# Moving the unit matrix and the ones to other start bytes in SBUF, in a two-layer decoder trunk

## The chip, the cores and the metric

The kernel runs on one core of one Trainium2 chip. The metric is the device time of one execution in microseconds (us), as the median of several runs of the same program.

## The reference

The input is one sequence of 256 tokens with 2048 channels in float32. Two layers follow each other: a gated DeltaNet layer (GDN) and an HGRN2 layer, each followed by a SwiGLU feed-forward part (FFN). Every part is normalised ahead and added to the residual, and a last normalisation ends the trunk.

```python
for layer in range(DEPTH):                      # DEPTH = 2
    if layer % N_MIXERS == 0:
        h = h + gdn_mixer(rmsnorm(h, gdn_norm[j]), ...)
    else:
        h = h + hgrn2_mixer(rmsnorm(h, hgrn_norm[j]), ...)
    h = h + swiglu(rmsnorm(h, ffn_norm[layer]), ...)
return rmsnorm(h, final_norm)
```

Both mixers project the normalised input with a large weight matrix, run a recurrence over the tokens in chunks of 64, normalise each head, multiply by a gate and project back with an output matrix. `swiglu` is `(silu(h @ w_gate) * (h @ w_up)) @ w_down`. Nearly all of the arithmetic lies in these products with weights.

## The kernel before, in words

All weights are read from HBM in pieces of 128x1024 float32 (`raw`). Each piece is split in two parts whose sum it is: ACT writes the high part `wh`, rounded to the type that TensorE takes in one pass (fp32r), and VectorE writes the low part `wl = raw - wh`. The activations are split in the same way (`xt_h`, `xt_l`; `hth`, `htl`; `ot_h`, `ot_l`). A product with weights is then three products on TensorE: high with high, high with low, low with high.

There are two ways in which the main stream issues them. `mm_rows` (L624) holds 128 tokens of the activations as the stationary operand and streams 512 columns of weights past it. `mm_cols` (L652) holds 128 columns of weights and streams all 256 tokens past them; it serves the projections whose results are wanted with channels on the partitions: `k` and `q` of the GDN layer and the first two of the four projections of each HGRN group. In the profile a product is named out<-moving,stationary, so `main<-xt_h,wh` with 256 columns is `mm_cols`, and `main<-wh,xt_h` with 512 columns is `mm_rows`. The weight buffers have their start bytes set by padding (`PAD`, `IN_COLS`, `make` at L446): 32 modulo 512 where weights are streamed, 108 (`wh`) and 364 (`wl`) where `mm_cols` holds them.

```python
PAD = 64
IN_COLS = {"wh": 108, "wl": 364}
```

Between the products of the main stream TensorE does small ones into other PSUM tiles (`aux`): the work of the recurrences, and transpositions. A transposition holds a 128x128 block of the data and streams the 128x128 unit matrix past it. `make_xt` (L716) transposes the layer's input `x` in this way, eight blocks at a time, four times for each of four norms; `head_out` (L1184) transposes the gated result `zs` of a head group, eight blocks at a time, for eight GDN groups and four HGRN groups:

```python
nc.tensor.transpose(
    tr[:, h * T + tt * P : h * T + (tt + 1) * P],
    zs[:, tt, (2 * b + h) * P : (2 * b + h + 1) * P], self.ident,
)
```

The unit matrix `self.ident` is the first 128 columns of the tile `head`, which is loaded once; its other 64 columns are norm weights. VectorE reads it too, to take diagonals (L1029) and to scale it into `vjunk` (L702). The tile `ones` is used by ten products that begin the program, as the stationary operand of four products with `vjunk` in two of the `make_rstd` calls (L705), and, one column of it, as the moving operand of the sums of squares in `gdn_qk` (L1024, `aux<-ones,sq`).

A recording layer keeps every operation, and a planner then puts all of them in an order, engine by engine, by its own costs and due times. The operations are issued from one line (L490), so that the profile shows this line for all of them, and groups are told apart by the names of their tiles. The constants lie in one pool and take their place in SBUF in the order in which `setup` (L535) declares them, each rounded up to 32 bytes per partition.

Of the kernel before, what the change touches and what calls it, by code (L numbers as in the profile page):

```python
# [17 lines left out]
P = 128  # L18
T = 256
# [487 lines left out]
class Trunk:  # L507
# [27 lines left out]
    def setup(self):  # L535
        nc, c = self.nc, self.const
        t = lambda shape, tag, dt=F32: self.tile(c, shape, tag, dt)
        self.x_home = self.tile(self.dram, [T, D], "x_home", bufs=1)
        self.x_at, self.x = self.a["x"], {}
        head = t([P, P + 64], "head")  # L540
        nc.sync.dma_start(head, self.a["head"])
        nc.ops[-1].lag = 2.4
        self.queue = [nc.ops[-1]]
        self.ident = head[:, 0:P]
        self.norms = head[:, P : P + 64].rearrange("p (n c) -> p n c", n=4)
        self.ones = t([P, P], "ones")
        nc.gpsimd.memset(self.ones, 1.0)
        self.neghalf = t([P, 8], "neghalf")
        nc.gpsimd.memset(self.neghalf, -0.5)
        self.rstd = t([P, 2], "rstd")  # L550
        self.rstdh = t([P, 2], "rstdh")
        self.rstd_row = t([P, T], "rstd_row")
        self.ssp = t([P, 2, 4], "ssp")
        self.ss = t([P, 2], "ss")
        self.junk = t([P, 512], "junk")
        self.vjunk = t([P, 256], "vjunk")
        self.xt_h = [t([P, 4, T], f"xt_h{i}", F32R) for i in range(4)]
        self.xt_l = [t([P, 4, T], f"xt_l{i}", F32R) for i in range(4)]

# [1201 lines left out]
```

## Time and profile before

| | |
|---|---|
| median of 3 runs | 2769.56 us (2769.43 to 2770.02) |
| profiled execution | 2768.12 us |
| its span, first to last instruction | 2766.0 us |
| mean granted TensorE clock | 0.999 |
| memory traffic | 580.52 MB by DMA, mean 210 GB/s |

The profile is of one execution. Busy times are sums over the span; products on TensorE overlap each other in the records, so that the distance from the start of one to the start of the next tells its price, not its own duration. The views used are the page's busy times and chain, the list of who waited for whom, the groups of instructions by name, the chain in order of time (merged pieces with their count), the timeline, and counts in chosen stretches. Times of day are us from the start of the span.

### The profile page before, as it was taken

How to read it: one execution, taken by the hardware profiler on the slowest of the kernel's cores; microseconds unless marked ns; L12 is line 12 of the kernel's file. 1: busy time of each engine (PE TensorE's matmuls, PEld its weight loads, DVE VectorE, ACT ScalarE, POOL GpSimd, SP SyncE). 2: the span in 40 equal slices, each digit the busy share in tenths (PEclk: the TensorE clock that was granted, in tenths of full speed). 3: DMA queues.
4: the chain of work that ended last, by engine and by line, in shares of the span. 5: the costliest groups of instructions: out<-in, count | busy, mean ns of one | idle time of the engine just before them, and what ended most of it. 6: DMA issues, size and time to landing. Idle time of an engine off the chain costs nothing.

```text
span 2766.0 us, 41091 instructions
## 1 busy us (share of the span) xinstructions
PE 2749.6 (99%) x15662; PEld 2333.5 (84%) x15662; DVE 1899.9 (69%) x2857; ACT 1428.6 (52%) x2010; POOL 251.6 (9%) x370
## 2 busy tenths in 40 slices
PE   9999999999999999999999999999999999999998
PEld 9888888888888888888888989988888888888887
DVE  7787888877766667446675688778657675456764
ACT  6646666565554444344444556556454444344443
POOL 1213222232110000000000100000100000000000
PEclk9999999999999999999999999999999999999999
DMA  7686668687776666676667655555776666766664
GB/s 262 201 282 222 189 213 286 205 276 218 229 254 202 193 194 194 224 223 195 192 191 224 219 163 175 168 166 176 231 258 195 193 193 209 224 208 194 195 200 160
DMA packets 162677, 580.52 MB, mean 210 GB/s; under 512 B 20138, under 2 KB 21306, under 8 KB 162352
## 3 DMA queue, kind: packets, MB, share of 16 engines
q1 hardware_dynamic: 138912, 503.15, 57.0%
q0 software_dynamic: 23280, 73.91, 8.5%
q8 instruction: 122, 2.00, 0.3%
q10 hardware_dynamic: 288, 0.85, 0.1%
q14 instruction: 75, 0.61, 0.1%
HBM read 550.52 MB, written 27.31 MB: 209 GB/s over the span
## 4 chain that ended last, share of the span: by engine, by line
PE 99%; ACT 0%; DVE 0%; issue 0%; DMA 0%; SPq 0%; POOLq 0%; POOL 0%; ACTq 0%
PE main L490 92%; PE aux L490 6%; ACT dec L490 0%; DMA first<-in_x 0%; DVE wl L490 0%; ACT wh L490 0%; DVE utmp L490 0%; SPq L490 0%; DVE pre L490 0%; ACT xt_h L490 0%; DVE u L490 0%; ACT y L490 0%; POOLq L1757 0%; ACT junk L490 0%; DVE xl L490 0%
## 5 line engine op out<-in xcount | busy, mean ns | idle before, releaser
L490 DVE TENSOR_TENSOR wl<-raw,wh 128x1024 fp32r<-128x1024 f32 x945 | 1160.7, 1229 | 755.6 <-ACT wh L490 742.2
L490 ACT ACTIVATE wh<-raw 128x1024 fp32r<-128x1024 f32 x945 | 1000.8, 1060 | 1226.9 <-PE main L490 1126.3
L490 PE MATMUL main<-wh,xt_h 128*128 128x512 f32 x2176 | 849.3, 390 | 0.8 <-ACT wh L490 0.8
L490 PE MATMUL main<-wl,xt_h 128*128 128x512 f32 x2176 | 848.4, 390 | 1.3 <-DVE wl L490 1.3
L490 PE MATMUL main<-wh,xt_l 128*128 128x512 f32 x2176 | 849.5, 390 | 0.0
L490 PEld LDWEIGHTS main<-wl,xt_h 128*128 128x128 f32 x2176 | 408.5, 188 | 85.7 <-DVE wl L490 1.6
L490 PEld LDWEIGHTS main<-wh,xt_h 128*128 128x128 f32 x2176 | 408.5, 188 | 85.0 <-ACT wh L490 1.2
L490 PEld LDWEIGHTS main<-wh,xt_l 128*128 128x128 f32 x2176 | 408.6, 188 | 84.4
L490 PE MATMUL main<-xt_h,wh 128*128 128x256 f32 (+1 forms) x1040 | 290.5, 279 | 0.7 <-ACT wh L490 0.7
L490 PE MATMUL main<-xt_h,wl 128*128 128x256 f32 (+1 forms) x1040 | 290.1, 279 | 1.0 <-DVE wl L490 0.9
L490 PE MATMUL main<-xt_l,wh 128*128 128x256 f32 (+1 forms) x1040 | 290.0, 279 | 0.3 <-DVE xt_l L490 0.3
L490 PE MATMUL main<-wh,htl 128*128 128x512 f32 x664 | 258.6, 389 | 0.0
L490 PE MATMUL main<-wl,hth 128*128 128x512 f32 x664 | 258.3, 389 | 0.0
L490 PE MATMUL main<-wh,hth 128*128 128x512 f32 x664 | 258.3, 389 | 0.0
L490 PEld LDWEIGHTS main<-xt_h,wl 128*128 128x128 f32 (+1 forms) x1040 | 194.5, 187 | 1.5 <-DVE wl L490 1.4
L490 PEld LDWEIGHTS main<-xt_h,wh 128*128 128x128 f32 (+1 forms) x1040 | 194.5, 187 | 1.3 <-ACT wh L490 0.9
L490 PEld LDWEIGHTS main<-xt_l,wh 128*128 128x128 f32 (+1 forms) x1040 | 194.5, 187 | 1.0 <-DVE xt_l L490 0.5
L490 DVE STREAM_TRANSPOSE turned<-h 32x256 f32<-32x256 f32 x352 | 153.5, 436 | 7.2
L490 PE MATMUL main<-wh,ot_l 128*128 128x512 f32 x384 | 151.2, 394 | 0.0
L490 PE MATMUL main<-wh,ot_h 128*128 128x512 f32 x384 | 150.6, 392 | 0.0
L490 PE MATMUL main<-wl,ot_h 128*128 128x512 f32 x384 | 150.5, 392 | 0.0
L490 PEld LDWEIGHTS main<-wh,hth 128*128 128x128 f32 x664 | 124.7, 188 | 25.9
(206 smaller groups left out, 2249.0 us busy)
## 6 DMA issues: line engine op xcount, KB each, us to landing
raw<-in_ffn_gu SPq DMA_DIRECT2D x352, 512.0 KB, 4.7
raw<-in_ffn_d SPq DMA_DIRECT2D x176, 512.0 KB, 4.7
raw<-in_hgrn_in SPq DMA_DIRECT2D x128, 512.0 KB, 4.1
raw<-in_gdn_kq SPq DMA_DIRECT2D x64, 512.0 KB, 5.4
raw<-in_gdn_v SPq DMA_DIRECT2D x64, 512.0 KB, 4.7
raw<-in_gdn_z SPq DMA_DIRECT2D x64, 512.0 KB, 4.9
raw<-in_gdn_out SPq DMA_DIRECT2D x64, 512.0 KB, 5.0
x_home<-x POOLq DMA_DIRECT2D x36, 512.0 KB, 6.7
```

What stands on the lines that cost most here:

```text
L490: getattr(getattr(tc.nc, op.eng), op.method)(*args, **kw)
```

## The change

`setup` declares the constants in another order and makes two of them larger, of which the kernel uses the same part as before. The tiles keep their contents; every instruction and its order on each engine stay. The place in SBUF changes, in bytes per partition, and with it the byte modulo 512:

| tile | first byte before (modulo 512) | after (modulo 512) |
|---|---|---|
| `head`, begins with the unit matrix | 16512 (128) | 16928 (32) |
| `ones` | 17280 (384) | 17696 (288) |
| `neghalf` | 17792 (384) | 16512 (128) |
| `rstd_row` | 17888 (480) | 18208 (288) |
| `junk` | 18976 (32) | 19232 (288) |
| `vjunk` | 21024 (32) | 21280 (288) |
| `rstd`, `rstdh`, `ssp`, `ss` | (416, 448, 480, 0) | (416, 448, 480, 0) |
| `xt_h0` and everything behind it | 22048 (32) and on | 512 bytes further, so the same |

```diff
@@ setup @@
         self.x_at, self.x = self.a["x"], {}
+        neghalf = t([P, 72], "neghalf")
+        self.neghalf = neghalf[:, 0:8]
+        self.rstd = t([P, 2], "rstd")
+        self.rstdh = t([P, 2], "rstdh")
+        self.ssp = t([P, 2, 4], "ssp")
+        self.ss = t([P, 2], "ss")
         head = t([P, P + 64], "head")
         nc.sync.dma_start(head, self.a["head"])
...
         self.ones = t([P, P], "ones")
         nc.gpsimd.memset(self.ones, 1.0)
-        self.neghalf = t([P, 8], "neghalf")
+        self.rstd_row = t([P, T], "rstd_row")
+        self.junk = t([P, 512], "junk")
+        self.vjunk = t([P, 320], "vjunk")[:, 0:256]
         nc.gpsimd.memset(self.neghalf, -0.5)
-        self.rstd = t([P, 2], "rstd")
-        self.rstdh = t([P, 2], "rstdh")
-        self.rstd_row = t([P, T], "rstd_row")
-        self.ssp = t([P, 2, 4], "ssp")
-        self.ss = t([P, 2], "ss")
-        self.junk = t([P, 512], "junk")
-        self.vjunk = t([P, 256], "vjunk")
         self.xt_h = [t([P, 4, T], f"xt_h{i}", F32R) for i in range(4)]
```

## The prediction

> **What bounds the kernel now.** I read the page's busy times and the chain first, then the waits, then TensorE's products one by one.
>
> ```profile
> span 2766.0 us, 41091 instructions
> PE 2749.6 (99%) x15662; PEld 2333.5 (84%) x15662; DVE 1899.9 (69%) x2857; ACT 1428.6 (52%) x2010; POOL 251.6 (9%) x370
> PE 99%; ACT 0%; DVE 0%; issue 0%; DMA 0%; SPq 0%; POOLq 0%; POOL 0%; ACTq 0%
> ```
>
> TensorE is busy 99% of the span, and the chain that ended last is TensorE's own queue. The list of who waited for whom says in which direction the weights are late:
>
> ```profile
> ACT wh L490 <- PE main L490: 1126.3, 754, 6.3
> PE main L490 <- DVE wl L490: 2.2, 2, 1.3
> ```
>
> ACT waits 1126.3 us, in 754 waits, for TensorE to hand back a weight buffer; TensorE's main stream waits 2.2 us for VectorE. What TensorE saves therefore reaches the end, unless the saving is more than the weights are ahead. So the question is whether a change of addresses alters the pace of TensorE's queue, and the chain in order of time shows that this pace isn't the same everywhere. Around the HGRN layer (start, length, piece, number of products):
>
> ```profile
> 1548.64 0.87 PE aux L490 x8
> 1549.51 7.20 PE main L490 x60
> 1556.71 0.44 PE aux L490 x4
> 1557.15 42.99 PE main L490 x338
> ...
> 1645.69 13.07 PE main L490 x115
> 1658.77 0.87 PE aux L490 x8
> 1659.64 40.62 PE main L490 x302
> ...
> 1759.75 40.62 PE main L490 x302
> ...
> 1859.87 40.62 PE main L490 x302
> ```
>
> In the pieces of 60 and 115 there are nothing but products of 256 columns (the stages that `mm_cols` issues): 7.20 us / 60 is 0.1200 us each, 13.07 / 115 is 0.1137. Same shape, same stage, 6% apart. The pieces of 302 and of 338 run from the 256-column stage into the next stage of 512 columns. The count of products in equal stretches inside the 256-column stages says the same (stretch; length, busy, products touched, granted clock, DMA share, GB/s):
>
> ```profile
> 1660.00:1690.00 30.00, 30.00 (x252) 1.00 0.58 181
> 1860.00:1890.00 30.00, 30.00 (x252) 1.00 0.57 180
> 1558.00:1588.00 30.00, 30.00 (x267) 1.00 0.66 212
> ```
>
> 252 against 267 products in 30 us (about two at the edges are counted with each): 0.1200 and 0.1132 us. The granted clock is 1.00 in all three, so it isn't the throttle, and TensorE is never idle, so it isn't a wait; the quicker stretch even has more DMA traffic. TensorE keeps one of two paces, for hundreds of products.
>
> What decides which? The timeline of TensorE where a slow stretch begins:
>
> ```profile
> 1658.60 1.04 PE L490 MATMUL aux<-head,zs 128*128 128x128 f32 x8
> 1659.40 0.36 PE L490 MATMUL main<-xt_h,wh 128*128 128x256 f32 x1
> 1659.60 0.28 PE L490 MATMUL main<-xt_l,wh 128*128 128x256 f32 x1
> 1659.72 0.28 PE L490 MATMUL main<-xt_h,wl 128*128 128x256 f32 x1
> 1659.84 0.28 PE L490 MATMUL main<-xt_h,wh 128*128 128x256 f32 x1
> ```
>
> and where another eight 128x128 products, `r` against `u`, come before the same first product:
>
> ```profile
> 225.33 1.05 PE L490 MATMUL aux<-r,u 128*128 128x128 f32 x8
> 226.13 0.36 PE L490 MATMUL main<-xt_h,wh 128*128 128x256 f32 x1
> 226.34 0.28 PE L490 MATMUL main<-xt_l,wh 128*128 128x256 f32 x1
> 226.46 0.28 PE L490 MATMUL main<-xt_h,wl 128*128 128x256 f32 x1
> 226.57 0.28 PE L490 MATMUL main<-xt_h,wh 128*128 128x256 f32 x1
> 226.69 0.28 PE L490 MATMUL main<-xt_l,wh 128*128 128x256 f32 x1
> 226.80 0.28 PE L490 MATMUL main<-xt_h,wl 128*128 128x256 f32 x1
> 226.91 0.28 PE L490 MATMUL main<-xt_h,wh 128*128 128x256 f32 x1
> ```
>
> After the eight transpositions (moving operand `head`, the unit matrix) the second start-to-start distance is 0.12 us and stays there. After `r,u` it is 0.12 once and then 0.11, 0.12, 0.11: 0.113 on average. The first distance is 0.20 in the one and 0.21 in the other. I went through every interruption of a 256-column stage: the slow pace holds in four stretches, and each begins right behind eight transpositions against the unit matrix (at 1549.3, 1659.4, 1759.5 and 1859.6 us); behind `r,u`, `w,nmat`, `w,dec`, `v,sc`, `ones,sq` and `vjunk,ones` it is gone within a handful of products. At 1556.71 four products of `vjunk` and `ones` even end a slow stretch. The moving operands of those that let go, but for the one-column `ones,sq`, begin at byte 32 modulo 256 in the built program; the unit matrix begins at 128.
>
> **The change, part by part.** What it adds and removes: no instruction, wait or transfer. It moves start bytes. The constants follow each other from byte 16512, each rounded up to 32 bytes: 288 + 4 x 32 ahead of `head` puts it at 16928, which is 32 modulo 512; `ones` follows 768 bytes later, at 288; `rstd_row`, `junk` and `vjunk` come to 288, and the 1280 bytes of `vjunk` bring everything behind it 512 bytes further, so to the same byte modulo 512 as before.
>
> *The slow stretches (the term that counts).* With the unit matrix at byte 32 the last transposition streams from the same place as `r` or `w` does, while the first weights of the stage are loaded. I take it that the start is then like theirs and the slow pace doesn't hold. The price comes by subtraction: the piece of 338 differs from the pieces of 302 by 36 more 256-column products at 0.1133 us, 4.08 us, and by its pace. So 302 products at its pace take 42.99 - 4.08 = 38.91 us, the way back to the quick pace included, where 40.62 stand now: 1.71 us, three times 5.13. The piece of 60 goes from 7.20 to 60 x 0.1133 + 0.03 = 6.83: 0.37. Sum: 5.50 us.
>
> *The transpositions themselves.* How many there are, and what eight cost beside eight `r,u`:
>
> ```profile
> L490 PE MATMUL aux<-head,x 128*128 128x128 f32 x112 | 14.5, 272 | 0.0
> L490 PE MATMUL aux<-head,zs 128*128 128x128 f32 x96 | 12.6, 273 | 0.0
> L490 PE MATMUL aux<-head,first 128*128 128x128 f32 x16 | 2.2, 279 | 1.3 <-DMA first<-in_x 1.3
> ...
> 225.49 0.89 PE aux L490 x8
> ```
>
> 224 transpositions in 28 groups of eight. Eight of them stand in the chain with 0.87 us, eight `r,u` (moving at byte 32, stationary at 32) with 0.89. If the new place brings them to that, it costs 28 x 0.02 = 0.56 us; no row shows a product of this size quicker, so a gain has no row behind it, and I bound it by the same 0.56. I take 0: their own row is the nearest, and `vjunk` on `ones`, whose stationary operand is elsewhere, takes the same as `r,u`, so the 0.02 seems to belong to their form.
>
> *Everything else that moved.* `ones` and `vjunk` as operands of TensorE go from 384 and 32 to 288; 288 is 32 modulo 256, and the weights of `mm_cols`, which lie at 108 and 364, 256 apart, keep one pace together, so I count 0. VectorE's and ACT's reads and writes of `rstd_row`, `junk` and `vjunk` are hidden by TensorE: ACT alone waits 1126.3 us for it. They would cost something only where TensorE waits, and there it waits 2.2 us in all for `wl`. The saving of 1.7 us a stretch uses up no lead either: the weights follow TensorE's own release of buffers.
>
> **Sum.** The profiled execution took 2768.12 us, 2.12 outside its span, and lies 1.44 below the median of the three runs, 2769.56. Minus 5.50 it comes to 2762.6 (span 2760.5), and the median to 2764.06, rounded 2764.1. With both ends for the transpositions: 2763.5 to 2764.6.
>
> The Trainium skill speaks against any effect: "SBUF — State Buffer", section "Who interferes with whom", gives TensorE two independent read ports, one for the moving operand and one for loading weights, and says that it never waits on anyone. By that rule the sum would be 0 and the time 2769.6. The trace doesn't agree with it as it stands: 0.1200 and 0.1132 us for one shape at one clock, with no wait.
>
> **The rivals.** *The form, not the place.* The slow pace could come from the transposition as such: its weight load takes 140 ns where that of `r,u` takes 191.
>
> ```profile
> L490 PEld LDWEIGHTS aux<-r,u 128*128 128x128 f32 x128 | 16.5, 191 | 1.0
> L490 PEld LDWEIGHTS aux<-head,zs 128*128 128x128 f32 x96 | 11.1, 140 | 1.2
> ```
>
> Form and place come together in all four stretches, so the trace of before can't part them. Then nothing changes: 2769.6, at most 0.56 either way. Against it: the slow pace hangs on a few ns in the first distance, and the moving operand's place is read at just that time. The rule of the Trainium skill's "SBUF — State Buffer" comes to the same time.
>
> *Only some let go.* The four starts read alike, so I expect all or none; should one long stretch stay, 2764.06 + 1.71 = 2765.8, with two 2767.5.
>
> *The slow pace moves to other starts.* `ones` and `vjunk` get new places as well, and stretches that now run quickly begin behind them:
>
> ```profile
> 33.62 11.58 PE main L490 x102
> ...
> 82.55 8.70 PE main L490 x75
> 92.78 6.32 PE main L490 x54
> 100.62 9.27 PE main L490 x80
> ```
>
> With the piece of 338 (297 of its products have 256 columns, since 42.99 us leave room for 41 of 512) these are some 610, and three like them further on, behind `ones,sq` in the same layer, add about 200. If they went slow, 810 x 0.0067 = 5.4 us would be added; without the gain, and with 0.56 for the transpositions, that is 2769.56 + 5.96 = 2775.5. The time rises from the point where more products are caught than the 843 (60 and three times 261) that are let go, and by 0.2% where about 750 are caught, the 0.56 comes on top and none is let go. Against it: 288 is 32 modulo 256.
>
> That the change doesn't do what it says I exclude by the sum of bytes above.
>
> **How the numbers follow.** A measurement of this kernel can tell about 0.2%, 5.5 us, from no change, so the line lies at 2764.02: my forecast falls almost on it. Forecast 0.76, some stretches 0.06, nothing 0.11, slower 0.07. Within the forecast I give the side beyond the line 0.42 and the side short of it 0.34: the re-entry cost is in the sum already, and a gain in the transpositions is as open as a loss. So faster 0.42, within 0.2% 0.34 + 0.06 + 0.11 = 0.51, slower 0.07. The range takes in the forecast with its bounds and 0.3 us of difference between sessions, 2763.2, and the case of two stretches that stay, 2767.5: 0.82 of the chance. The forecast's own range is 2763.2 to 2764.9.
>
> **What would show it.** In the chain of the changed kernel the three pieces of 302 shrink from 40.62 to 38.9 us and the piece of 60 from 7.20 to 6.8; 30 us inside them hold 267 products, not 252; the first distance behind the transpositions is 0.21 and the pace behind it 0.113. The transpositions stay at 0.87 us for eight (0.89 would show the collision). I am wrong if the pieces of 302 still take 40.62 (then it is the form), or if pieces behind `ones` or `vjunk` grow, 42.99 to 45.0 the largest.

## The result, and the profile after

The changed kernel takes 2763.82 us (median of 15 runs, 2762.36 to 2766.25), the kernel before 2769.43 us in the same comparison (15 runs, 2767.86 to 2771.01). The ratio is 0.998, with a 95% interval of 0.9972 to 0.9988: 5.61 us faster, 0.203%. (Of the ten runs of the first experiment below, one took 4631.39 us at a granted clock of 0.556; its median is that of the other nine.)

The chain in order of time of the changed kernel, at the same places as in the prediction (start, length, piece, count of products):

```profile
1549.53 0.87 PE aux L490 x8
1550.40 6.81 PE main L490 x60
1557.21 0.44 PE aux L490 x4
1557.65 43.01 PE main L490 x338
...
1646.21 13.07 PE main L490 x115
1659.28 0.87 PE aux L490 x8
1660.16 38.91 PE main L490 x302
...
1758.56 38.91 PE main L490 x302
...
1856.96 38.91 PE main L490 x302
```

The three pieces of 302 products fell from 40.62 to 38.91 us and the piece of 60 from 7.20 to 6.81: 3 x 1.71 + 0.39 = 5.52 us. The pieces of 115 and 338, which were quick before, have the lengths they had (13.07, and 43.01 against 42.99), and eight transpositions still stand with 0.87. The timeline of TensorE at the first of the three starts:

```profile
1659.12 1.04 PE L490 MATMUL aux<-head,zs 128*128 128x128 f32 x8
1659.91 0.36 PE L490 MATMUL main<-xt_h,wh 128*128 128x256 f32 x1
1660.12 0.28 PE L490 MATMUL main<-xt_l,wh 128*128 128x256 f32 x1
1660.23 0.28 PE L490 MATMUL main<-xt_h,wl 128*128 128x256 f32 x1
1660.34 0.28 PE L490 MATMUL main<-xt_h,wh 128*128 128x256 f32 x1
1660.45 0.28 PE L490 MATMUL main<-xt_l,wh 128*128 128x256 f32 x1
1660.57 0.28 PE L490 MATMUL main<-xt_h,wl 128*128 128x256 f32 x1
```

Behind the transpositions the first distance is 0.21 us where it was 0.20, and the next ones are 0.11 at once. The trace keeps the starts to the nanosecond: 199 and then 122 ns before, 202 and then 113 now. A start that differs by so little goes with a pace that differs by 6.7 ns for the 259 products behind it.

The profiled execution has a span of 2761.4 us, 4.6 less than before, not 5.5. Most of the rest was lost at the start, in work that the change doesn't touch: the load of the first block of `x`. In the chain of the changed kernel it holds the end up for

```profile
2.21 6.53 DMA first<-in_x
```

and in that of the kernel before for

```profile
2.21 5.67 DMA first<-in_x
```

That is 0.86 us of a load that differs from run to run (6.27 us in the kernel with `vjunk` at 128, below). At the first long piece, of 144 products, 0.64 us of it is left (17.23 us against 16.59); another 0.25 is lost in small steps up to 1549 us, whose cause wasn't looked into.

### The profile page after: what moved, and what is told of

It reads as the page before. It is cut to its first block, busy times and chain, and to the rows that moved or that the text cites. A ratio compares the mean times of both kernels' runs of the same rounds, so it can differ in the third digit from the quotient of the medians.

```text
span 2761.4 us, 41091 instructions
## 1 busy us (share of the span) xinstructions
PE 2744.9 (99%) x15662; PEld 2328.7 (84%) x15662; DVE 1899.6 (69%) x2857; ACT 1428.3 (52%) x2010; POOL 251.4 (9%) x370
## 4 chain that ended last, share of the span: by engine, by line
PE 98%; ACT 0%; DVE 0%; issue 0%; DMA 0%; SPq 0%; POOLq 0%; POOL 0%; ACTq 0%
PE main L490 92%; PE aux L490 6%; DMA first<-in_x 0%; ACT dec L490 0%; DVE wl L490 0%; ACT wh L490 0%; DVE utmp L490 0%; SPq L490 0%; DVE pre L490 0%; ACT xt_h L490 0%; DVE u L490 0%; ACT y L490 0%; POOLq L1758 0%; ACT junk L490 0%; DVE xl L490 0%
## 5 line engine op out<-in xcount | busy, mean ns | idle before, releaser
L490 PEld LDWEIGHTS main<-wl,hth 128*128 128x128 f32 x664 | 124.6, 188 | 25.9
```

The source lines that it names most:

```text
L490: getattr(getattr(tc.nc, op.eng), op.method)(*args, **kw)
```

## The experiments

Two theories stood against each other. Mine: where the transposition streams the unit matrix from decides whether the stage behind it falls into the slow pace. Its rivals: the gain comes from `ones`, `vjunk` and the others, or the transposition's form makes the slow pace and the place has nothing to do with it. Where only one time is given it is of one run, and only its profile is argued from, but for the last experiment, where the time is used as well and this is said.

**The unit matrix alone.** The kernel before, with `head` moved from byte 128 to 32 modulo 512. The norm weights behind the unit matrix in the same tile move with it, and `neghalf`, which only GpSimd (POOL) reads, goes from 384 to 128. Every other constant stays at its old byte modulo 512.

```diff
+        self.neghalf = t([P, 104], "neghalf")[:, 0:8]
-        head = t([P, P + 64], "head")
+        head = t([P, 216], "head")[:, 0 : P + 64]
...
-        self.ones = t([P, P], "ones")
+        self.ones = t([P, 136], "ones")[:, 0:P]
-        self.neghalf = t([P, 8], "neghalf")
```

> Only the unit matrix goes to byte 32 modulo 512; ones stay at 384, vjunk at 32, rstd_row at 480, junk at 32, as before. Theory (the moving operand's place in the last transposition decides the pace that follows): all of the gain, the three pieces of 302 products at 38.91 us, the piece of 60 at 6.81, the time about 2764. Rival (ones, vjunk or the other constants bring the gain): pieces at 40.62 and 7.20, about 2769.5. If the gain is shared, something between.

Measured: 2764.58 us, the median of nine runs, against 2768.46 in the same comparison; ratio 0.9984 (0.9974 to 0.9993). The chain has the quick pieces:

```profile
1551.37 6.81 PE main L490 x60
...
1661.12 38.91 PE main L490 x302
...
1857.92 38.91 PE main L490 x302
```

**Everything but the unit matrix.** The changed kernel, with `head` back at byte 128 modulo 512 and `ones` and what follows left where the change puts them.

```diff
-        self.ss = t([P, 2], "ss")
-        head = t([P, P + 64], "head")
+        self.ss = t([P, 32], "ss")[:, 0:2]
+        head = t([P, 296], "head")[:, 0 : P + 64]
```

> The other half: the unit matrix stays at byte 128 modulo 512, while ones, rstd_row, junk and vjunk go to 288 and the order of declaration is that of the changed kernel. Theory: nothing gained, pieces of 302 at 40.62 us, piece of 60 at 7.20, about 2769.5. Rival (the other constants, or the new order, bring it): 38.91 and about 2764.

Measured: 2769.33 us, ratio 1.0002 (0.9993 to 1.0012), and the old pieces:

```profile
1551.30 7.19 PE main L490 x60
...
1661.44 40.62 PE main L490 x302
...
1861.67 40.62 PE main L490 x302
```

By the pieces the unit matrix brings all of the gain: they are those of the changed kernel in the one and those of the kernel before in the other. The times agree, though by themselves they are too coarse to say "all": 3.9 us between the medians of the first experiment, 2 to 7 by its interval. The order of declaration and the other constants change nothing clear of the spread.

**A map of places.** The changed kernel with the unit matrix at six other bytes modulo 512. The edit is the one just shown, with other widths, so that `ones` stays at 288.

> The changed kernel with the unit matrix at byte 288 modulo 512 (32 modulo 256). Theory with a period of 256 bytes, as the weights at 108 and 364 suggest: as the changed kernel, pieces of 302 at 38.91 us, about 2764. Rival (period of 512, so that 288 is as foreign as 128): the slow pace, 40.62 and about 2769.

> The changed kernel with the unit matrix at byte 64 modulo 512. If only a place equal to that of the main stream's operands (32 modulo 256) lets go: pieces of 302 at 40.62 us, about 2769. If 128 alone is the unlucky place, because the slow pace needs one certain first distance: 38.91, about 2763.8.

> The changed kernel with the unit matrix at byte 96 modulo 512, between 64, which let go after a few products, and 128, which holds the slow pace. First distance behind the transpositions 201 or 202 ns: quick, pieces of 302 at 38.9 us. 199 ns: slow, 40.62. No forecast between the two.

> The changed kernel with the unit matrix at byte 160 modulo 512. As for byte 64: 40.62 us and about 2769 if only 32 modulo 256 lets go; 38.91 and about 2763.8 if the slow pace needs one certain first distance that 128 happened to give. 160 is the neighbour of 128, so of the tried places the likeliest to be caught as well.

> The changed kernel with the unit matrix at byte 224 modulo 512. As for byte 64: 40.62 us and about 2769 if only 32 modulo 256 lets go; 38.91 and about 2763.8 if 128 is an unlucky single place.

> The changed kernel with the unit matrix at byte 256 modulo 512, between 224 (slow) and 288 (quick), and a round number that a layout might choose. If the slow places are those from 128 to 224: quick, 38.9 us. If only the places just above 32 modulo 256 let go: slow, 40.62.

The first of the three long pieces in the chain, in the order 64, 96, 160, 224, 256, 288:

```profile
1659.95 38.92 PE main L490 x302
```

```profile
1659.39 38.91 PE main L490 x302
```

```profile
1659.66 40.62 PE main L490 x302
```

```profile
1661.20 40.62 PE main L490 x302
```

```profile
1661.04 38.91 PE main L490 x302
```

```profile
1659.44 38.91 PE main L490 x302
```

| byte of the unit matrix, modulo 512 | 32 | 64 | 96 | 128 | 160 | 224 | 256 | 288 |
|---|---|---|---|---|---|---|---|---|
| piece of 302 products, us | 38.91 | 38.92 | 38.91 | 40.62 | 40.62 | 40.62 | 38.91 | 38.91 |
| time of the one run, us | (above) | 2763.25 | 2762.65 | (above) | 2767.70 | 2769.54 | 2764.24 | 2763.01 |

So neither reading of the map that I had put down holds. 128 isn't a single unlucky place, since 160 and 224 are as slow; nor is 32 modulo 256 the only good one, since 64, 96 and 256 are as quick. Of the places tried, those from 128 to 224 are slow and the others quick. 288, a quarter of a kilobyte behind 32, behaves as 32 does; whether 384, the partner of 128, is slow wasn't tried, so a period of 256 is not shown. That it is the byte modulo 512 that counts rests on one pair: in the kernel before the unit matrix begins at byte 16512, in the second experiment at 17024, and both are slow.

The map is that of four stages that `mm_cols` issues, with their weights at 108 and 364; it doesn't hold for every stage. Near the start of the program eight transpositions stand ahead of `mm_gates`, which also issues products of 256 columns but holds 64 columns of weights, at 32 modulo 256 (`128*64` in the timeline). In the kernel before, with the unit matrix at 128:

```profile
12.09 1.03 PE L490 MATMUL aux<-head,x 128*128 128x128 f32 x8
...
14.01 0.28 PE L490 MATMUL main<-xt_h,wh 128*64 128x256 f32 x1
...
15.93 0.28 PE L490 MATMUL main<-xt_h,wl 128*64 128x256 f32 x1
```

In the changed kernel, with it at 32:

```profile
8.78 1.10 PE L490 MATMUL aux<-head,first 128*128 128x128 f32 x8 [1.45 <-DMA first<-in_x]
...
9.84 0.28 PE L490 MATMUL main<-xt_l,wh 128*64 128x256 f32 x1
...
10.79 0.28 PE L490 MATMUL main<-xt_h,wh 128*64 128x256 f32 x1
```

The first has 17 distances in 1.92 us, 0.113 each, from the tenth product behind the transpositions on; the second has 8 in 0.95 us, 0.119 each, up to its end. Byte 128 isn't slow as such, then, nor is 32 quick as such.

**Another product streamed from byte 128.** The changed kernel with `vjunk`, the moving operand of four ordinary products, at 128.

```diff
-        self.junk = t([P, 512], "junk")
-        self.vjunk = t([P, 320], "vjunk")[:, 0:256]
+        self.junk = t([P, 600], "junk")[:, 0:512]
+        self.vjunk = t([P, 360], "vjunk")[:, 0:256]
```

> The changed kernel with vjunk, the moving operand of the four products with ones, at byte 128 modulo 512 instead of 288; the unit matrix stays at 32. Theory (place alone decides, whatever the form of the product): the two stretches behind vjunk go slow, the piece of 338 from 43.01 to about 45.0 us and the piece of 102 near the start from 11.6 to about 12.2; together 2.6 us more, about 2766.4. Rival (a transposition's form is needed as well): they stay at 43.0 and 11.6, about 2763.8.

Measured: 2765.64 us; the pieces behind `vjunk` are as they were. The one of 102 products near the start takes 11.60 us (11.59 in the changed kernel). The one in the HGRN layer, in the chain:

```profile
1559.87 43.02 PE main L490 x338
```

The timeline at its start:

```profile
1559.26 0.60 PE L490 MATMUL aux<-vjunk,ones 128*128 128x128 f32 x4
1559.62 0.37 PE L490 MATMUL main<-xt_h,wh 128*128 128x256 f32 x1
1559.83 0.28 PE L490 MATMUL main<-xt_l,wh 128*128 128x256 f32 x1
1559.94 0.28 PE L490 MATMUL main<-xt_h,wl 128*128 128x256 f32 x1
1560.06 0.28 PE L490 MATMUL main<-xt_h,wh 128*128 128x256 f32 x1
```

The first distance is 0.21 and the stage returns to the quick pace. My theory, that the place decides whatever the product's form, fell here: byte 128 is harmless for these ordinary products.

**The same operands in the other form.** The kernel before, with the HGRN groups' transpositions issued as ordinary products with the unit matrix.

```diff
@@ head_out, behind each transposition @@
+                    if isinstance(scale, float):
+                        nc.ops[-1].share = -1.0
@@ issue @@
+                if op.method == "transpose" and op.share < 0:
+                    tc.nc.tensor.matmul(*args, start=True, stop=True)
+                    continue
```

> The kernel before, unit matrix at byte 128, but the 32 transpositions of the four HGRN groups are issued as ordinary products with the unit matrix (the same operands, place and order; two passes where a transposition takes one, so about 0.11 us more each, 3.5 us in all). The transpositions of x ahead of the piece of 60 stay as they are. If the form counts beside the place: pieces of 302 at 38.9 us, piece of 60 still at 7.20; time about 2769.5 + 3.5 - 5.1 = 2768. If the place alone counted: pieces of 302 at 40.62, about 2773.

Measured: 2766.98 us. In the chain (L491 is the line that issues the ordinary products):

```profile
1549.06 0.87 PE aux L493 x8
1549.93 7.20 PE main L493 x60
...
1659.18 1.78 PE aux L491 x16
1660.96 38.94 PE main L493 x302
```

The piece of 60, whose transpositions were left as they were, is slow; the pieces of 302, with the unit matrix at the same byte 128, are quick. So in this stage form and place are needed together: change either, and the slow pace is gone. The form can't be parted from its timing here: an ordinary product of this type stands in the trace as two records (16 for eight products), so that the run-up to the stage gets longer too, 1.78 us against 0.87.

**Only one of the eight.** The same kernel with one ordinary product in each group of eight. By the planner's order it is the last of the eight in the first two groups, and the fifth in the third.

```diff
@@ head_out, behind the loops over the transpositions @@
+        if isinstance(scale, float):
+            nc.ops[-1].share = -1.0
```

> The kernel before, unit matrix at byte 128; of each HGRN group's eight transpositions one is issued as an ordinary product. In the first two groups that lead into a slow stretch it is the very last of the eight, in the third it is the fifth, with three transpositions behind it. If only the last product before the stage sets its pace: the first two pieces of 302 at about 38.9 us, the third at 40.62, the piece of 60 (its transpositions untouched) at 7.20; time about 2769.5 - 3.4 + 0.4 = 2766.5. If all eight count, or their mean: either none or all three change.

Measured: 2764.04 us. All three long pieces went quick, the third too:

```profile
1550.22 7.20 PE main L493 x60
...
1660.46 38.91 PE main L493 x302
...
1758.98 38.91 PE main L493 x302
...
1857.49 38.91 PE main L493 x302
```

The third start in the timeline:

```profile
1856.34 0.60 PE L493 MATMUL aux<-head,zs 128*128 128x128 f32 x4
1856.78 0.39 PE L491 MATMUL aux<-head,zs 128*128 128x128 f32 x2
1857.00 0.49 PE L493 MATMUL aux<-head,zs 128*128 128x128 f32 x3
1857.24 0.36 PE L493 MATMUL main<-xt_h,wh 128*128 128x256 f32 x1
1857.45 0.28 PE L493 MATMUL main<-xt_l,wh 128*128 128x256 f32 x1
1857.56 0.28 PE L493 MATMUL main<-xt_h,wl 128*128 128x256 f32 x1
```

Here three transpositions from byte 128 come right ahead of the stage, just as in the kernel before, and yet the first distance is 0.21 and the next 0.11. The last product ahead of the stage doesn't set the pace by itself, nor do the last three: one ordinary product four places earlier is enough to change it. I read this as the stage inheriting the timing of the whole run-up; the runs don't show by what.

**The other side of the distance.** The kernel before, with the weights of `mm_cols` moved by 96 bytes, so that they lie as far behind the unit matrix as in the changed kernel.

```diff
-IN_COLS = {"wh": 108, "wl": 364}
+IN_COLS = {"wh": 204, "wl": 460}
```

> The kernel before, unit matrix at byte 128, with the weights that mm_cols holds moved by 96 bytes, from 108 and 364 to 204 and 460, so that they lie as far behind the unit matrix as they do in the changed kernel. If the distance between the last moving operand and the next weights decides, and the stage keeps its quick pace: pieces of 302 at 38.9 us, piece of 60 at 6.8. If the unit matrix's own place decides: 40.62 and 7.20. The stage's own pace may change too, because its moving operand stays at 32: then the pieces behind other products (115 products in 13.07 us) are the measure of that, up to 13.8 if all of them go slow.

Measured: 2780.31 us, 10 us slower than the kernel before beside it (2770.27, one run each).

```profile
1566.79 44.60 PE main L490 x338
...
1656.96 13.67 PE main L490 x115
1671.51 40.34 PE main L490 x302
```

The whole stage changed its pace: 115 products behind other work take 13.67 us instead of 13.07, 0.1189 each, and the piece of 302 at 40.34 belongs to the same pace. The start behind the transpositions can't be read from it any more, so the run says nothing on the distance between unit matrix and weights. What it does show, in one run, is that the quick pace itself depends on where the weights lie: at 204 and 460 the stage has neither 0.113 nor 0.120.

## Why the prediction was right

*What bounds.* TensorE's queue did, and what it saved reached the end: 5.52 us in the chain's pieces, 5.61 between the medians. That the two agree to 0.1 us is in part chance: the profiled execution shows 4.6, and single runs of the changed kernel lie up to 3.9 us apart.

*The slow stretches.* Forecast 38.91 and 6.83 us, measured 38.91 and 6.81. The subtraction of a quick piece from a slow one held to 0.02 us. The 0.03 that the 6.83 included for a way back to the pace wasn't spent, since there was no way back: 60 x 0.1133 is 6.80.

*The transpositions.* Forecast 0 from their own row, with 0.56 either way: eight of them still take 0.87. The "eight `r,u`" beside them were misread: an ordinary product stands as two records, so x8 are four products (and x4 of `vjunk,ones` two). The difference of 0.02 us is between records, and the forecast doesn't hang on it.

*The rest.* `ones` and `vjunk` at 288 were counted at 0. The experiment that moved them without the unit matrix gives a ratio of 1.0002 (0.9993 to 1.0012).

*The reason given.* It was right about the object and too simple about the cause, and that the forecast came out all the same is in part luck. Byte 32 was chosen as the place of `r` and `w`; that isn't why it is quick, since 64, 96 and 256 are as quick, and with five of eight places quick the choice would often have come right without the reason. I wrote that the last transposition would then stream from the same place as `r` or `w`, and that the start would be like theirs. The place does decide for a transposition (32 against 128, with all else equal), but not by itself: an ordinary product from 128 lets go, and so do eight transpositions with one ordinary product among them. Nor does the start become like that behind `r,u`: there the second distance was 0.12, here it is 0.11 at once. And the few ns in the first distance don't part the two paces: to the nanosecond, at these four starts in the profiles of all kernels here but the last, the 18 slow ones have 199 or 200 and the 34 quick ones 200 to 205. The second distance does part them, 121 or 122 against 113 to 118. The count of starts also left out `mm_gates`, where eight transpositions from byte 128 let go in the kernel before.

*The rivals.* "The form, not the place" was half right: the form, or the timing that comes with it, is needed too, which the trace of before couldn't tell, since form and place came together in all four stretches. "Only some let go": all four did. "The slow pace moves to other starts": the piece of 338 stands at 43.01, none was caught. The same stage has three paces (0.113, 0.119, 0.120) by nothing but start bytes. The Trainium skill's "SBUF — State Buffer", section "Who interferes with whom", has two independent read ports and a TensorE that never waits on anyone, by which the change would have given 0; these runs don't agree with that.

*The line.* The forecast lay 0.04 us short of the 0.2% line and the measurement 0.07 beyond it; that close, on which side it came is luck: the interval of the measurement, 0.12 to 0.28%, has the line in its middle.

What stays open is why the slow pace takes hold behind transpositions from 128 to 224 and not behind those from 32 to 96 and 256 to 288, and whether the place acts through their timing. The runs show the places and the few ns at the start, not what collides.

## What to carry to other kernels

Where one shape runs at two paces with no wait and at one clock, count the products in equal stretches and look at what stands ahead of each slow one: a pace that holds itself can be traced to its start, and is priced by subtracting a quick piece from a slow one. Then try the start byte of the small operand ahead of it, alone, before touching the main stream; here it costs nothing and three of eight places were bad. Which places are bad has to be measured for each stage; the map above isn't a rule. Don't move the main stream's operands by the same argument without a run: moving the weights by 96 bytes cost nearly twice what the unit matrix gained (10 us, from one run, against 5.6).

## What the runs showed of the hardware that I had not expected

- TensorE's products of 256 columns have a quick and a slow pace, 0.1133 and 0.1200 us. The slow one held for 259 products, to the end of the stage, behind a start that differs from a quick one by 3 ns in the first distance and 9 ns in the second (199 and 122 against 202 and 113).
- What comes further back than the last product counts: one ordinary product, four places ahead of the stage, turned a slow stretch into a quick one.
- The place of the stationary operand modulo 512 moves the stage's own pace: 108 and 364 give 0.113, 204 and 460 give 0.119 (one run), with the moving operand at 32 in both.
